# Attention of an encoder's first layer: items taken in pairs at set times instead of spread evenly

## The chip, the cores and the metric

The kernel runs on one core of a Trainium2 chip. The metric is the device time of one execution in microseconds (us), as the median of several runs. Engines are named as in the profile: PE (TensorE, matmuls and transposes; PEld is its weight load), DVE (VectorE), ACT (ScalarE), POOL (GpSimd), SP (SyncE, which issues the transfers).

## The reference

256 tokens of 1024 channels pass through two layers and a final norm; all is float32. The change is in the first ("even") layer, which runs two attentions side by side and projects both to the output:

```python
def even_mixer(xn, w_in, rpb, q_norm, w_uq, kv_norm, w_ukv, w_o, cos_r, sin_r):
    hcat = xn @ w_in
    a_qkv = hcat[..., :o0].reshape(b, s, 3, NA_HEADS, HEAD_DIM)
    out_a = neighbourhood_attention(a_qkv[:, :, 0], a_qkv[:, :, 1], a_qkv[:, :, 2], rpb)
    c_q = rms_norm(hcat[..., o0:o1], q_norm)
    c_kv = rms_norm(hcat[..., o1:o2], kv_norm)
    k_pe = apply_rope(hcat[..., o2:][:, :, None, :], cos_r, sin_r)
    q = (c_q @ w_uq).reshape(b, s, MLA_HEADS, MLA_NOPE + MLA_ROPE)
    q = jnp.concatenate([q[..., :MLA_NOPE], apply_rope(q[..., MLA_NOPE:], cos_r, sin_r)], axis=-1)
    kv = (c_kv @ w_ukv).reshape(b, s, MLA_HEADS, MLA_NOPE + MLA_V)
    ...
    out_b = dense_attention(q, k, v, (MLA_NOPE + MLA_ROPE) ** -0.5)
    return jnp.concatenate([out_a, out_b], axis=-1) @ w_o
```

Both attentions have 8 heads. The kernel computes the neighbourhood attention densely, with a bias table that carries the window; the other one ("MLA") has 96 channels per head for queries and keys and 64 for values. The second ("odd") layer and the two MLP blocks are as before in both kernels and come after the stretch that is changed.

## The kernel before

**Products.** A float32 operand is cut into a high half and the rest: `split` writes the high half on ACT (a CAST, L181) and the rest on DVE (a subtraction, L182). One product is then three matmuls (`mm3`, L185 to L187). `two_heads` (L194) does the same for two heads of 64 channels at once: they stand in two halves of PE's rows, which the trace shows as a 64*128 tile. The mix (L757) writes two heads into two halves of PE's columns, a 128*64 tile. All other matmuls and the transposes use the full array (128*128, or 96*128).

**Items.** The 16 items of the attention are 2 kinds x 4 pairs of heads x 2 tiles of 128 tokens. One item is: scores on PE; sn (a scaled copy and its row minimum) on DVE, L728 or L731; Exp on ACT, L733, one for each head; the reciprocal rz on DVE, L734; the scaling on ACT, L736, one for each head; four transposes on PE (`turn_probs`, L743); a copy of them to `pts` on ACT or DVE (L745), whichever the scheduler picks; the mix on PE (L757); and the split of the mix into oah/oal (first kind) or obh/obl (second kind), the operands of the output projection.

**Around them.** `main` lists the GEMM steps of the stretch with a cost in us each: the query and key projections of head pairs 1 to 3 (`qk_steps`), the MLA's up-projections (`kg`, `ug`: GEMM, copies to ktok and qtok, rotary embedding on DVE, L517 to L521) and their transposes (`kt`, `ut`, L649, split into kh/kl and qh/ql), and the first part of the output projection (`out_steps`). Its sum of costs serves as a clock: after each step the loop issues as many entries of `side`, the list of scores, turns and mixes, as keeps both lists in step. In `side` the scores of item n stand before the turn of item n-1 and the mix of item n-2. A scheduler then puts the instructions of each engine in a fixed order; `tc.high_priority` moves those inside it ahead. The banks of PSUM come from two tags, "acc" and "w"; the weights are split on ACT and DVE some steps ahead (whi, wlo).

Of the kernel before, what the change touches and what calls it, by code (L numbers as in the profile page):

```python
# [23 lines left out]
P = 128  # L24
D = 1024
KT = D // P
T = 256
NT = T // P
# [10 lines left out]
SPLIT_AHEAD = 2  # L39
WPARTS = 4  # L40
NORM_PRIO = 300

QK_ORDER = (0, 2, 1)

# [2 lines left out]
def trunk(ctx, tc, a, out):  # L47
    nc = tc.nc
# [8 lines left out]
    def scratch(shape, name):  # L57

        n = int(np.prod(shape))
        v = work.tile([P, 512], F32, tag="scratch", name=name, bufs=12)[:, :n]  # L60
        if len(shape) == 2:
            v = v.rearrange("p (a b) -> p a b", b=shape[1])
        return v
# [10 lines left out]
    def quarter_pair(name):  # L74
        return [act.tile([P, KT // 2, T], F32R, tag="quarter", name=name + v, bufs=4) for v in "hl"]

    def bank(tag):
        return ps.tile([P, 512], F32, tag=tag, name=tag)
# [101 lines left out]
    def split(hi, lo, src, eng=None):  # L180
        a = nc.scalar.copy(hi, src).ins  # L181
        return a, (eng or nc.vector).tensor_tensor(lo, src, hi.bitcast(F32), op=ALU.subtract).ins  # L182

    def mm3(o, sh, sl, mh, ml, first, last):
        nc.tensor.matmul(o, sh, mh, start=first, stop=False)  # L185
        nc.tensor.matmul(o, sh, ml, start=False, stop=False)  # L186
        nc.tensor.matmul(o, sl, mh, start=False, stop=last)  # L187

    def two_heads(o, hi, lo, ts):

        for n, (y, z) in enumerate(((hi, hi), (hi, lo), (lo, hi))):
            for j in range(2):
                pb = slice(64 * j, 64 * j + 64)
                nc.tensor.matmul(o[j], y[pb, 0, ts], z[pb, 1, :], start=n == 0, stop=n == 2)  # L194
# [10 lines left out]
    def tok(t):  # L205
        return slice(t * P, (t + 1) * P)
# [61 lines left out]
    def column(r, t):  # L268
        return r[:, t:t + 1]
# [8 lines left out]
    def join(b, o, n, xT):  # L278

        v = x[:, 2 * b:2 * b + 2, :]  # L280
        nc.vector.tensor_tensor(v, two(o), v, op=ALU.add)
        for f in zip(*(prepare(k, n, xT) for k in (2 * b, 2 * b + 1))):
            run_all(f)

    def hand_over(accs, last, n):

        xT, s = pair_tile(), sum_tile()
        for b in range(4):
            last[b]()
            with tc.high_priority(NORM_PRIO):  # L290
                join(b, accs[b], n, xT)
        return xT, s

    def hand_over_tokens(accs, last, n, scale):
# [4 lines left out]
        def leave(h, t):  # L299
            last(h, t)  # L300
            acc, sc = accs[2 * t + h], column(scale, t)
            with tc.high_priority(NORM_PRIO):
                y = ys[h, t] = scratch([512], "y")
# [3 lines left out]
        def turn(h):  # L307
            with tc.high_priority(NORM_PRIO):
                for b in range(2):
                    pt = bank("w")  # L310
                    for k in range(2):
                        for t in range(NT):
                            c = (2 * b + k) * P
                            nc.tensor.transpose(pt[:, k * T + t * P:k * T + (t + 1) * P], ys[h, t][:, c:c + P], ident)
                    join(2 * h + b, pt, n, xT)
# [21 lines left out]
    def out_steps(accs, mixed, wo, k):  # L337

        def step(fbs):
            if k // 2 not in wo:  # L340
                wo[k // 2] = weight()
            onto(accs, wo[k // 2], (k % 2) * D, (ALL, k % 4), mixed[k // 4], k == 0, k == KT - 1, fbs)
        return [lambda fbs=fbs: step(fbs) for fbs in (range(0, 4), range(4, 8))]
# [148 lines left out]
    def even(ep):  # L492
# [205 lines left out]


        mixed = [quarter_pair("oa"), None]  # L700
        items = [(0, t, hp) for hp in range(4) for t in range(NT)] + [(1, t, hp) for hp in range(4) for t in range(NT)]
        biases, probs, turned = {}, {}, {}

        def load_bias(n):
            if n < 8:
                _, t, hp = items[n]
                biases[n] = ep.tile([P, 2, T], F32, tag="bias", name="bias", bufs=2)
                nc.sync.dma_start(biases[n], a["rpb"][t, hp])

        def scores(n):  # L710
            kind, t, hp = items[n]
            load_bias(n + 2)

            sb = [bank("w")[:, 0:T] for _ in range(2)] if kind == 0 else bank("w").rearrange("p (j n) -> p j n", j=2)
            s_of = lambda j: sb[j] if kind == 0 else sb[:, j]
            if kind == 0:
                two_heads(sb, *qk[hp], tok(t))
            else:
                for j in range(2):
                    h = 2 * hp + j  # L720
                    (qh, ql), (kh, kl) = mT["q"], mT["k"]
                    mm3(sb[:, j], qh[0:96, h, tok(t)], ql[0:96, h, tok(t)], kh[0:96, h, :], kl[0:96, h, :], True, True)
            pp, sn = scratch([2, T], "pp"), scratch([2, T], "sn")
            mn, z, rz = (work.tile([P, 2], F32, tag=v, name=v, bufs=3) for v in ("mn", "z", "rz"))
            for j in range(2):
                o = s_of(j)
                if kind == 0:
                    nc.vector.tensor_tensor_reduce(out=sn[:, j], in0=o, in1=biases[n][:, j, :], op0=ALU.add, op1=ALU.min,  # L728
                                                   scale=-1.0, scalar=3e38, accum_out=mn[:, j:j + 1])
                else:  # L730
                    nc.vector.tensor_scalar(sn[:, j], o, -MLA_SCALE, None, ALU.mult, ALU.min, accum_out=mn[:, j:j + 1])  # L731
            for j in range(2):
                nc.scalar.activation(pp[:, j], sn[:, j], AF.Exp, bias=mn[:, j:j + 1], scale=-1.0, accum_out=z[:, j:j + 1])  # L733
            nc.vector.reciprocal(rz, z)  # L734
            for j in range(2):
                nc.scalar.activation(pp[:, j], pp[:, j], AF.Copy, scale=rz[:, j:j + 1])  # L736
            probs[n] = pp

        def turn_probs(n):
            pp = probs.pop(n)  # L740
            pt = bank("w")
            for b in range(4):
                nc.tensor.transpose(pt[:, b * P:(b + 1) * P], pp[:, b // 2, (b % 2) * P:(b % 2 + 1) * P], ident)  # L743
            turned[n] = scratch([4, P], "pts")
            nc.any.tensor_copy(out=turned[n], in_=pt.rearrange("p (b n) -> p b n", b=4))  # L745

        def mix(n):
            kind, t, hp = items[n]
            pts = turned.pop(n)
            if mixed[kind] is None:  # L750
                mixed[kind] = quarter_pair("ob")
            v = (vna, vml)[kind]
            pvo = bank("acc" if n < 6 else "w")
            for kk in range(NT):
                for j in range(2):
                    h = 2 * hp + j
                    nc.tensor.matmul(pvo[64 * j:64 * j + 64, 0:P], v[:, kk, h * 64:(h + 1) * 64], pts[:, 2 * j + kk, :],  # L757
                                     start=kk == 0, stop=kk == NT - 1)
            split(*(z[:, hp, tok(t)] for z in mixed[kind]), pvo[:, 0:P])

        def attention():

            out = []
            for n in range(len(items) + 2):
                for fn, m in ((scores, n), (turn_probs, n - 1), (mix, n - 2)):
                    if 0 <= m < len(items):
                        out.append(lambda fn=fn, m=m: fn(m))
                if n == 0:
                    out += [lambda: None] * 2
            return out  # L770

        (ug, ut), (kg, kt) = uq_steps(), ukv_steps()
        first = qk_steps(0)
# [12 lines left out]
        main = [(1.31, f) for c in range(1, 4) for f in qk_steps(c)]  # L786
# [4 lines left out]
                     (.98, ug[i(1, h)]), (.43, kt[i(1, h)]), (.43, ut[i(1, h)])]  # L791
        main += [(0, lambda: accs.extend(open_accs()))]
        main += [(1.3, f) for k in range(6) for f in out_steps(accs, mixed, wo, k)]
        side = attention()
        at = -5
        total = sum(c for c, _ in main) + at
        done = 0
        for c, f in main:
            f()
            at += c  # L800
            while done < len(side) and done * total < at * len(side):
                side[done]()
                done += 1
        return accs, out_last(accs, mixed, wo)


    def odd(op, xT, s):
# [46 lines left out]
        def qk_steps(d):  # L854
# [4 lines left out]
            def gemm(b, f, half):  # L859
# [9 lines left out]
                if half == 1:  # L869
                    with tc.high_priority(NORM_PRIO):  # L870
                        if f == 0:
# [40 lines left out]
        def attention(u, d):  # L912
# [36 lines left out]
            def mix(out_tag):  # L949
                pvo = [bank(out_tag) for _ in range(NT)]  # L950
                for i in range(NT):
# [4 lines left out]
                    for c in range(2):  # L956
                        qs = slice(64 * c, 64 * c + 64)
                        for j in range(2):
                            cs = slice(64 * j, 64 * j + 64)
                            nc.tensor.matmul(pvo[i][cs, qs], d["v12"][:, 2 * i + c, cs], turned[i, j][:, 2, qs], start=False, stop=c == 1)  # L960
                with tc.high_priority(NORM_PRIO):
                    for i in range(NT):
# [37 lines left out]
        mix = done.pop()  # L1000
        weave(qk_steps(nd) + all_values(nd, NORM_PRIO), steps + [nothing, lambda: mix("w")])
        steps = attend(7, nd)
# [111 lines left out]
```

## Time and profile before

| | before |
|---|---|
| median of 3 runs | 747.87 us (747.73 to 748.14) |
| profiled execution | 748.65 us |
| its span | 746.9 us |
| PE busy in the span | 739.0 us |
| DVE busy, ACT busy | 544.2 us, 484.8 us |
| the attention stretch | 39.3 to 108.6 us of the span |

The span is the time from the first to the last recorded instruction of the profiled execution; 1.75 us lie around it. The attention stretch runs from the first scores to the last mix. A start is counted from the beginning of the span. In a timeline the time from one instruction's start to the next one's (its pitch) tells more than the duration, since neighbours overlap.

### The profile page before, as it was taken

Reading aid. Unit: us, or ns where it says so; the run is one execution under the profiler, and the core shown is the slowest. Engines: PE = TensorE matmul, PEld = TensorE weight load, DVE = VectorE, ACT = ScalarE, POOL = GpSimd, SP = SyncE. Lnnn points to the kernel's source line nnn. Section 1 sums busy time; section 2 is a strip of 40 time slices with the busy share of each in tenths; the row PEclk is TensorE's granted clock in tenths of the full one; section 3 lists DMA queues with packets and bytes.
Section 4 is the critical chain, followed back from the end, with each engine's and each line's share of the span. In section 5 each row is a group of like instructions: output and inputs, shape, how many; then the busy total and the mean of one; then the engine's idle time right before and its main releaser. Section 6 shows DMA issues by size and latency. Waiting matters only on the chain.

```text
span 746.9 us, 12279 instructions
## 1 busy us (share of the span) xinstructions
PE 739.0 (99%) x4635; PEld 646.4 (87%) x4635; DVE 544.2 (73%) x1137; ACT 484.8 (65%) x1075; POOL 8.7 (1%) x20
## 2 busy tenths in 40 slices
PE   9999999999999999999999999999999999999996
PEld 6998998888888888889899899998998888888885
DVE  6778858766566666997888788888858765665664
ACT  6788967554554555677786877867856554554551
POOL 0100000000000001000000000000000000000000
PEclk9999999999999999999999999999999999999998
DMA  8763334464555545554645636445545555545501
GB/s 282 317 255 114 114 113 170 171 225 173 179 211 177 186 172 165 200 183 165 208 141 178 223 122 215 165 162 198 203 165 176 190 198 197 186 183 187 193 15 56
DMA packets 25163, 133.19 MB, mean 178 GB/s; under 512 B 3728, under 2 KB 4752, under 8 KB 12304
## 3 DMA queue, kind: packets, MB, share of 16 engines
q1 hardware_dynamic: 24960, 132.15, 50.1%
q8 instruction: 36, 0.59, 0.3%
q10 hardware_dynamic: 144, 0.26, 0.1%
q14 instruction: 23, 0.19, 0.1%
HBM read 127.16 MB, written 1.05 MB: 172 GB/s over the span
## 4 chain that ended last, share of the span: by engine, by line
PE 93%; DMA 3%; DVE 1%; issue 1%; SPq 1%; ACT 1%; POOL 0%; POOLq 0%; ACTq 0%
PE w L370 16%; PE acc L185 14%; PE acc L187 13%; PE acc L186 13%; PE acc L867 12%; PE w L371 8%; PE acc L868 6%; PE w L194 1%; PE w L945 1%; PE w L925 1%; PE w L743 1%; DMA gx<-in_gx 1%; DMA bias<-in_rpb 1%; DMA raw<-in_w_v 1%; PE w L757 1%
## 5 line engine op out<-in xcount | busy, mean ns | idle before, releaser
L182 DVE TENSOR_TENSOR wlo<-raw,whi 128x512 fp32r<-128x512 f32 (+3 forms) x487 | 306.6, 664 | 135.1 <-ACT whi L181 134.4
L181 ACT CAST whi<-raw 128x512 fp32r<-128x512 f32 (+3 forms) x487 | 264.3, 601 | 171.3 <-PE w L370 62.3
L370 PE MATMUL w<-pair,whi 128*128 128x512 f32 x512 | 182.2, 397 | 0.0
L371 PE MATMUL w<-pair,wlo 128*128 128x256 f32 x512 | 143.9, 281 | 0.0
L867 PE MATMUL acc<-pair,whi 128*128 128x512 f32 x384 | 139.4, 403 | 0.0
L370 PEld LDWEIGHTS w<-pair,whi 128*128 128x128 f32 x512 | 96.2, 188 | 23.2
L868 PE MATMUL acc<-pair,wlo 128*128 128x256 f32 x384 | 108.1, 282 | 0.0
L185 PE MATMUL acc<-whi,hh 128*128 128x512 f32 x250 | 98.1, 392 | 0.0
L187 PE MATMUL acc<-whi,hl 128*128 128x512 f32 x250 | 97.7, 391 | 0.0
L186 PE MATMUL acc<-wlo,hh 128*128 128x512 f32 x250 | 97.7, 391 | 0.0
L371 PEld LDWEIGHTS w<-pair,wlo 128*128 128x128 f32 x512 | 96.1, 188 | 0.9
L867 PEld LDWEIGHTS acc<-pair,whi 128*128 128x128 f32 x384 | 72.2, 188 | 16.2
L868 PEld LDWEIGHTS acc<-pair,wlo 128*128 128x128 f32 x384 | 72.2, 188 | 0.2 <-issue 0.2
L187 PEld LDWEIGHTS acc<-whi,hl 128*128 128x128 f32 x250 | 47.0, 188 | 9.9
L185 PEld LDWEIGHTS acc<-whi,hh 128*128 128x128 f32 x250 | 47.0, 188 | 9.8
L186 PEld LDWEIGHTS acc<-wlo,hh 128*128 128x128 f32 x250 | 47.0, 188 | 8.9
L185 PE MATMUL acc<-whi,pair 128*128 128x384 f32 x128 | 43.8, 342 | 0.0
L187 PE MATMUL acc<-whi,pair 128*128 128x384 f32 x128 | 43.1, 337 | 0.0
L186 PE MATMUL acc<-wlo,pair 128*128 128x384 f32 x128 | 43.1, 337 | 0.0
L374 ACT COPY side<-w 128x256 f32<-128x256 f32 x64 | 23.7, 370 | 22.1 <-PE w L371 22.1
L375 DVE TENSOR_TENSOR u<-w,side 128x256 f32<-128x256 f32 x64 | 27.0, 421 | 3.8 <-ACT side L374 3.0
L181 ACT CAST hh<-hsq 128x512 fp32r<-128x512 f32 x32 | 19.9, 621 | 10.2 <-DVE hsq L377 10.2
(215 smaller groups left out, 1112.3 us busy)
## 6 DMA issues: line engine op xcount, KB each, us to landing
raw<-in_w SPq DMA_DIRECT2D x64, 1024.0 KB, 4.8
raw<-in_w_oqk SPq DMA_DIRECT2D x24, 1024.0 KB, 5.0
raw<-in_w_ov SPq DMA_DIRECT2D x16, 768.0 KB, 4.4
raw<-in_w_qk SPq DMA_DIRECT2D x4, 1024.0 KB, 8.9
raw<-in_w_oe SPq DMA_DIRECT2D x4, 1024.0 KB, 5.2
sw<-qk SPq DMA_DIRECT2D x64, 64.0 KB, 2.4
raw<-in_w_oo SPq DMA_DIRECT2D x4, 1024.0 KB, 5.1
bias<-in_rpb SPq DMA_DIRECT2D x8, 256.0 KB, 4.2
```

Source lines behind the costliest of these rows:

```text
L181: a = nc.scalar.copy(hi, src).ins
L182: return a, (eng or nc.vector).tensor_tensor(lo, src, hi.bitcast(F32), op=ALU.subtract).ins
L185: nc.tensor.matmul(o, sh, mh, start=first, stop=False)
L186: nc.tensor.matmul(o, sh, ml, start=False, stop=False)
L187: nc.tensor.matmul(o, sl, mh, start=False, stop=last)
L194: nc.tensor.matmul(o[j], y[pb, 0, ts], z[pb, 1, :], start=n == 0, stop=n == 2)
L370: nc.tensor.matmul(two(pu[f]), w[0][:, c], xT[2][:, k], start=k == 0, stop=False)
L371: nc.tensor.matmul(pu[f][:, 0:T], w[1][:, c], xT[0][:, k, :], start=False, stop=k == KT - 1)
L374: nc.scalar.copy(side[:, f], pu[f][:, T:2 * T])
L375: nc.vector.tensor_tensor(u[:, f], pu[f][:, 0:T], side[:, f], op=ALU.add)
L867: nc.tensor.matmul(two(pq), wh[:, ws], xp[:, k], start=k == 0, stop=False)
L868: nc.tensor.matmul(pq[:, 0:T], wl[:, ws], xh[:, k, :], start=False, stop=k == KT - 1)
```

## The change

The items are ordered so that the two tiles of one pair of heads follow each other, as before, but eight times are written out by hand. At the time `PAIRS_AT[p]` of the clock of `main` the scores of both tiles of pair p are issued, then the mix of both tiles of pair p-1 into one bank of 256 columns, and one split of 128x256 in place of two of 128x128; that split is issued with high priority. The turns of the two tiles follow 2.0 and 3.2 us of the clock later.

```diff
+PAIRS_AT = (5.0, 9.2, 13.6, 18.0, 22.6, 26.9, 31.1, 35.2)
+PAIRS_END = 39.6
...
-        def mix(n):
-            kind, t, hp = items[n]
-            pts = turned.pop(n)
+        def mix(p, tag):
+
+            kind, _, hp = items[2 * p]
...
-            pvo = bank("acc" if n < 6 else "w")
-            for kk in range(NT):
-                for j in range(2):
-                    h = 2 * hp + j
-                    nc.tensor.matmul(pvo[64 * j:64 * j + 64, 0:P], v[:, kk, h * 64:(h + 1) * 64], pts[:, 2 * j + kk, :],
-                                     start=kk == 0, stop=kk == NT - 1)
-            split(*(z[:, hp, tok(t)] for z in mixed[kind]), pvo[:, 0:P])
+            pvo = bank(tag)
+            for n in (2 * p, 2 * p + 1):
+                pts, tk = turned.pop(n), tok(items[n][1])
+                for kk in range(NT):
+                    for j in range(2):
+                        h = 2 * hp + j
+                        nc.tensor.matmul(pvo[64 * j:64 * j + 64, tk], v[:, kk, h * 64:(h + 1) * 64], pts[:, 2 * j + kk, :],
+                                         start=kk == 0, stop=kk == NT - 1)
+            with tc.high_priority(NORM_PRIO):
+                split(*(z[:, hp, :] for z in mixed[kind]), pvo[:, 0:T])
...
-            for n in range(len(items) + 2):
-                for fn, m in ((scores, n), (turn_probs, n - 1), (mix, n - 2)):
-                    if 0 <= m < len(items):
-                        out.append(lambda fn=fn, m=m: fn(m))
-                if n == 0:
-                    out += [lambda: None] * 2
-            return out
+            for p, at in enumerate(PAIRS_AT):
+                tag = "acc" if p < 5 else "w"
+
+                def start(p=p, tag=tag):
+                    for n in (2 * p, 2 * p + 1):
+                        scores(n)
+                    if p:
+                        mix(p - 1, tag)
+                out.append((at, start))
+                out += [(at + d, lambda n=2 * p + k: turn_probs(n)) for k, d in enumerate((2.0, 3.2))]
+            return out + [(PAIRS_END, lambda: mix(len(PAIRS_AT) - 1, "w"))]
...
-        side = attention()
-        at = -5
-        total = sum(c for c, _ in main) + at
-        done = 0
+        side, at = attention(), 0
         for c, f in main:
             f()
             at += c
-            while done < len(side) and done * total < at * len(side):
-                side[done]()
-                done += 1
+            while side and side[0][0] <= at:
+                side.pop(0)[1]()
```

The lines behind the new constants stand 3 lower than before (L194 becomes L197, L743 becomes L746, L733 and L736 become L736 and L739), and the mix is L762 instead of L757. The number of PE's instructions is the same; ACT has 6 fewer and DVE 10 fewer. Behind the attention every engine's order is the same.

On PE, an item of the first pairs stood alone before. These rows of the kernel before are the mix of item 1 and the scores of item 4, with the projection's matmuls around them.

```order
L185 MATMUL acc<-pair,whi 128x256
L186 MATMUL acc<-pair,whi 128x256
L187 MATMUL acc<-pair,wlo 128x256
L757 MATMUL acc<-pts,vna 64x128 x4
L194 MATMUL w<-qk_h 128x256 x2
L194 MATMUL w<-qk_l,qk_h 128x256 x2
L194 MATMUL w<-qk_h,qk_l 128x256 x2
L185 MATMUL acc<-pair,whi 128x256
```

In the changed kernel the scores of pair 2 (items 4 and 5) and the mix of pair 1 make one block on PE:

```order
L197 MATMUL w<-qk_h 128x256 x2
L197 MATMUL w<-qk_l,qk_h 128x256 x2
L197 MATMUL w<-qk_h,qk_l 128x256 x2
L197 MATMUL w<-qk_h 128x256 x2
L197 MATMUL w<-qk_l,qk_h 128x256 x2
L197 MATMUL w<-qk_h,qk_l 128x256 x2
L762 MATMUL acc<-pts,vna 64x128 x8
L188 MATMUL acc<-pair,whi 128x256
```

So twelve score matmuls and eight of the mix now stand together, where each item's six and four stood apart.

One pair later, on PE, the block of pair 3 (the scores of items 6 and 7, and the mix of pair 2) does not stay together in the changed kernel. The MLA's up-projections (384 columns) and single matmuls of scores and mix alternate:

```order
L197 MATMUL w<-qk_h,qk_l 128x256 x2
L762 MATMUL acc<-pts,vna 64x128 x4
L188 MATMUL acc<-whi,ch 128x384
...
L197 MATMUL w<-qk_h 128x256
L197 MATMUL w<-qk_l,qk_h 128x256
L197 MATMUL w<-qk_h,qk_l 128x256
L762 MATMUL acc<-pts,vna 64x128
L197 MATMUL w<-qk_h 128x256
L197 MATMUL w<-qk_l,qk_h 128x256
L197 MATMUL w<-qk_h,qk_l 128x256
L762 MATMUL acc<-pts,vna 64x128 x3
```

The second item's scores are issued one head at a time there, and the mix in pieces of 4, 1 and 3 matmuls. Then come the rest of the up-projections with eight transposes (L652), and the turns of items 6 and 7:

```order
L190 MATMUL acc<-whi,cl 128x384
L746 MATMUL w<-ident,pp 128x128 x4
L652 MATMUL w<-ident,qtok 96x128 x4
L746 MATMUL w<-ident,pp 128x128 x4
L652 MATMUL w<-ident,ktok 96x128 x4
L188 MATMUL w<-kh,qh 128x256
```

Between the two turns stands the transpose of qtok (L652), which was not next to them before; no main matmul is left between them and the first MLA scores (L188, kh and qh).

On ACT, at the same place in the kernel before (numbers behind a name tell buffers apart), the split's cast of one item and then the Exp of the next item:

```order
L181 CAST kh_858<-w_931 96x4x128 [waits PE_49]
L181 CAST oah_370<-acc_960 128x128 [waits PE_49]
L733 ACTIVATE pp_919,z_922<-sn_920,mn_921 128x256 [waits DVE_49] x2
L689 COPY ktok_942<-acc_938 128x4x64
L181 CAST qh_887<-w_953 96x4x128 [waits PE_49]
L667 COPY qtok_974<-acc_967 128x4x64 [waits PE_49]
L736 ACTIVATE pp_919<-pp_919,rz_923 128x256 [waits DVE_49]
```

And in the changed kernel, from the last rows before the cast of pair 2's mix to the scaling of item 7 (935 is item 6, 955 is item 7):

```order
L692 COPY ktok_923<-acc_919 128x4x64 [waits PE_49]
L184 CAST oah_370<-acc_967 128x256 [waits PE_49]
L736 ACTIVATE pp_935,z_938<-sn_936,mn_937 128x256 [waits DVE_49] x2
L184 CAST qh_888<-w_978 96x4x128 [waits PE_49]
L736 ACTIVATE pp_955,z_958<-sn_956,mn_957 128x256 [waits DVE_49,Activation_49]
L739 ACTIVATE pp_935<-pp_935,rz_939 128x256 [waits DVE_49]
L739 ACTIVATE pp_935<-pp_935,rz_939 128x256 [waits Activation_49]
L736 ACTIVATE pp_955,z_958<-sn_956,mn_957 128x256
L670 COPY qtok_992<-acc_985 128x4x64
L184 CAST kh_866<-w_1000 96x4x128 [waits PE_49]
L739 ACTIVATE pp_955<-pp_955,rz_959 128x256 [waits DVE_49]
```

The cast waits for the whole mix of pair 2 and stands ahead of all four Exps of pair 3; the copy qtok_992, which the transpose between the two turns needs, stands behind them.

## Rows read from the trace of the kernel before

**Rows 1.** The page: busy time of the engines, and the chain that ended last.

```profile
PE 739.0 (99%) x4635; PEld 646.4 (87%) x4635; DVE 544.2 (73%) x1137; ACT 484.8 (65%) x1075; POOL 8.7 (1%) x20
...
PE 93%; DMA 3%; DVE 1%; issue 1%; SPq 1%; ACT 1%; POOL 0%; POOLq 0%; ACTq 0%
```

**Rows 2.** Windows: stretch, its length, busy us, granted clock, DMA share, GB/s.

```profile
39.30:108.60 69.30, 69.30 (x597) 60.87 (x596) 53.18 (x170) 58.79 (x168) 1.17 (x4) 1.00 0.44 160
730.00:747.00 17.00, 10.88 (x65) 9.54 (x64) 7.43 (x15) 3.36 (x9) 1.22 (x2) 0.88 0.16 62
```

**Rows 3.** Timeline of PE (start, duration): scores between full-array matmuls.

```profile
39.00 0.28 PE L186 MATMUL acc<-pair,whi 128*128 128x256 f32 x1
39.11 0.28 PE L187 MATMUL acc<-pair,wlo 128*128 128x256 f32 x1
39.31 0.38 PE L194 MATMUL w<-qk_h 64*128 64x256 f32 x2
...
39.86 0.38 PE L185 MATMUL acc<-pair,whi 128*128 128x256 f32 x1
40.09 0.28 PE L186 MATMUL acc<-pair,whi 128*128 128x256 f32 x1
```

**Rows 4.** Timeline of PE: a mix and scores behind it, without a break.

```profile
52.48 0.28 PE L187 MATMUL acc<-pair,wlo 128*128 128x256 f32 x1
52.69 0.66 PE L757 MATMUL acc<-pts,vna 128*64 128x128 f32 x8
53.28 0.38 PE L194 MATMUL w<-qk_h 64*128 64x256 f32 x2
...
53.82 0.38 PE L185 MATMUL acc<-pair,whi 128*128 128x256 f32 x1
```

**Rows 5.** Timeline of PE: a mix in two pieces, then one in a piece.

```profile
82.84 0.43 PE L757 MATMUL w<-pts,vml 128*64 128x128 f32 x2
83.20 0.44 PE L743 MATMUL w<-ident,pp 128*128 128x128 f32 x2
83.57 0.65 PE L757 MATMUL w<-pts,vml 128*64 128x128 f32 x6
84.15 0.39 PE L185 MATMUL w<-kh,qh 96*128 96x256 f32 x1
...
87.13 0.66 PE L757 MATMUL w<-pts,vml 128*64 128x128 f32 x8
87.71 0.39 PE L185 MATMUL w<-kh,qh 96*128 96x256 f32 x1
```

**Rows 6.** Timelines, one item: its scores on PE, its first sn on DVE.

```profile
45.37 0.39 PE L194 MATMUL w<-qk_h 64*128 64x256 f32 x2
...
46.10 0.42 DVE L728 CUSTOM_DVE_ANT_0 sn<-w,bias 128x256 f32<-128x256 f32 x1
```

**Rows 7.** Timeline of ACT; the bracket is the idle time before, and what ended it.

```profile
39.35 1.02 ACT L181 CAST whi<-raw 128x256 fp32r<-128x256 f32 x3 [0.23 <-ACT whi L181]
...
64.41 0.27 ACT L181 CAST oah<-acc 128x128 fp32r<-128x128 f32 x1 [0.66 <-PE acc L757]
64.57 0.51 ACT L733 ACTIVATE pp<-sn,mn 128x256 f32<-128x256 f32 x1
...
65.07 0.50 ACT L733 ACTIVATE pp<-sn,mn 128x256 f32<-128x256 f32 x1
...
65.82 0.59 ACT L181 CAST qh<-w 96x512 fp32r<-96x512 f32 x1
66.29 0.38 ACT L667 COPY qtok<-acc 128x256 f32<-128x256 f32 x1
66.56 0.92 ACT L736 ACTIVATE pp<-pp,rz 128x256 f32<-128x256 f32 x2
```

**Rows 8.** Timeline of DVE: rest of kh, then a rotary embedding up to the next sn.

```profile
64.06 0.68 DVE L182 TENSOR_TENSOR kl<-w,kh 96x512 fp32r<-96x512 f32 x1
...
67.04 0.28 DVE L517 TENSOR_TENSOR r<-acc,cosr 128x128 f32<-128x128 f32 x1
...
67.50 0.41 DVE L728 CUSTOM_DVE_ANT_0 sn<-w,bias 128x256 f32<-128x256 f32 x1
```

More of the change, by code (lines that the diff above doesn't have):

```diff
@@ L700, in even @@
         mixed = [quarter_pair("oa"), None]
-        items = [(0, t, hp) for hp in range(4) for t in range(NT)] + [(1, t, hp) for hp in range(4) for t in range(NT)]
+        items = [(kind, t, hp) for kind in range(2) for hp in range(4) for t in range(NT)]
         biases, probs, turned = {}, {}, {}
@@ L800, in even @@
             at += c
-            while done < len(side) and done * total < at * len(side):
-                side[done]()
-                done += 1
+            while side and side[0][0] <= at:
+                side.pop(0)[1]()
+        assert not side
         return accs, out_last(accs, mixed, wo)
```

## The prediction

> **What bounds the kernel now.** I read the page first. PE is busy 739.0 of 746.9 us, and 93% of the chain that ended last is PE's [rows 1]. Then the windows: in the stretch of the attention, 39.3 to 108.6 us, PE is busy all 69.30 us at a granted clock of 1.00, while ACT has 58.79 and DVE 53.18 us of work [rows 2]. So PE sets the time of this stretch, and ACT and DVE matter only where they let PE wait, which they don't do now. Behind the stretch PE's order is unchanged and it has nothing to make up for a delay, so that I let what PE gains or loses here shift the end one for one. The change must pay in PE's own time, and may cost in waits that don't exist yet.
>
> PE's matmuls are the same before and after. What differs is how often it changes the shape of its tiles, so I read PE's timeline next, from start to start.
>
> **What it removes: changes of tile shape.** A full-array matmul of 256 columns takes .11 us (39.00 to 39.11). Before scores it takes .20 (39.11 to 39.31), the six of them take .55 (39.31 to 39.86) where three pairs, two heads in parallel, would be .34 at .11, and the first full one behind them takes .23 (39.86 to 40.09) [rows 3]. So an excursion to the scores' shape costs .09 + .21 + .12 = **.42 us** more than its work. For the mix: .21 before it (52.48 to 52.69), .59 for it (52.69 to 53.28) [rows 4] or .58 (87.13 to 87.71) [rows 5] where four pairs at .11 would be .44; with .11 behind it, as behind the scores, it makes .10 + .15 + .11 = **.36 us**. Mix and scores in a row share one exit: .10 from the full shape, .15 in the mix, then .54 instead of .34 for the scores (53.28 to 53.82) [rows 4] and .12 behind them, in all **.57 us**. A mix that is cut in two leaves a matmul without its partner: .36 (82.84 to 83.20) and .58 (83.57 to 84.15) [rows 5], .94 instead of .58; beside the second entry and exit that is .21 to .22 of lost parallel work.
>
> Before, 5 scores stand alone, 3 stand behind a mix, and 12 mixes stand alone, with one more in two pieces: 5 x .42 + 3 x .57 + 14 x .36 is 8.85 us, near the 9.0 that I get with the changes inside one block counted one by one. After, pair 0 is one excursion (.42), pairs 1 and 2 are scores with a mix behind them (.57 each), pair 3 and its mix make six alternations (scores with mix .57, then scores, mix, scores and mix of .3 to .4 each), and pair 4 cuts its mix in two, pair 5 too, and pairs 6 to 8 have one mix each. I count 30 changes against 47, 6.3 us with .8 of work that loses its partner. **The removal is worth 9.0 - 6.3 = 2.7 us.** A sum of what each block of the stretch takes above its nominal pitches gives 10.6 us, of which 1.6 belongs to other things; I take 2.7 and no more.
>
> The splits: 16 of 128x128 become 8 of 128x256. On ACT that is .16 each (64.41 to 64.57) against .31 (three in .93 and one overlap, 1.02) [rows 7], so nothing to be gained; on DVE a little. ACT and DVE are off the path, so this counts as nothing, hidden by PE's 69.3 us against their 58.8 and 53.2 [rows 2]. If that cover were gone it would still be worth under 1 us in all.
>
> **What it adds: the softmax of two items at once.** In pairs 0 to 2 both items' scores end within 1.1 us, and four Exps at .50 (64.57 to 65.07) and four scalings at .41 (two in .92) [rows 7] follow, with the cast of the mix, .31, ahead of them. The first sn starts .73 behind the scores' start (45.37 to 46.10) and takes .42 [rows 6]. That makes the first transposes possible about .73 + .42 + two or three Exps + .31 + other casts, 3.6 to 3.7 us behind the pair's first score, with the second half .41 later; PE, with the matmuls that stand between at .11 each, comes there after 3.5 to 3.8. That is too close to tell. The bounds for each of the six turns are 0 (the scaling is ready) and .5 (PE comes as the first scaling starts, and waits for a whole one); I take the middle, .25, for **1.5 us**.
>
> **Pair 3** is where I find a real wait. ACT's row there has the cast of pair 2's mix ahead of all Exps of pair 3. PE reaches the end of that mix late, because the order puts up-projections between its pieces: from the turn of item 5 to the mix's end I add four transposes at .11, three matmuls of 512 columns at .23 and five of 384 at .17 (by columns, from .11 for 256), three blocks of scores at .55 [rows 3] and the mix's pieces at .36, .36 and .58 [rows 5], with two entries from the full shape at .20: 5.1 by these, and 5.5 with the exits, which I take. ACT's work from there is kh (.47, 65.82 to 66.29), pts about the same, qtok .27 (66.29 to 66.56) and two ktok near it [rows 7], and three casts of weights near .52, in all 3.3 us. So ACT stands about 2 us at the cast, with Exps behind it whose sn is there. The row of before shows the same wait in small: the cast of 64.41 was preceded by .66 us of idle time, ended by PE's mix, and the Exp started right behind it, at 64.57 [rows 7].
>
> From the start of that cast on, ACT runs cast .31, two Exps (1.3), qh .47 (1.8), the third Exp (2.3), two scalings (3.1), the fourth Exp (3.6), qtok (3.9), kh (4.4). DVE then has the reciprocal of item 7, r1 and r2 (.46, 67.04 to 67.50), the rest of kh (.68) [rows 8] and only then the sum that finishes qtok, so this is there at 5.3. PE meanwhile has 2.9 us of other work (seven matmuls of 384 columns, three of 512, eight transposes, one exit), turns item 6 at 2.8 to 3.5 with a wait of .25, and then wants the transposes of qtok: **PE waits about 1.85 us** there, with nothing else in its row. What is queued behind it: the turn of item 7 and the transposes of ktok, then the MLA's scores, so everything shifts. Bounds: nothing, if ACT is itself so late that it comes to the cast with the mix; 2.5, if kl takes DVE first and the cast starts with the mix's end.
>
> The Trainium skill, in Perfetto Trace Analysis, section Tensor Engine Instruction, says that PE may pull weight loads ahead but that ACT and DVE run strictly in order. By that rule the Exps stay behind the cast and the sum holds; were they able to pass it, the 1.85 would fall away and the sum would be near -1.2. The idle time of 64.41 agrees with the rule [rows 7], and the sum goes by that row.
>
> In the second half, pairs 4 to 8, I find .3 us: the turn of item 8 is ready 3.06 after the mix of pair 3, and PE comes after 3.15.
>
> **The sum** on the profiled execution's own 748.65 us (its span of 746.9 and 1.75 around): -2.7 + 1.5 + .25 + 1.85 + .3 = +1.2. Since PE's blocks ran 1.6 us longer than the pitches that I added, ACT gets that time too; I give back .5 of it: **+0.7 us**, 749.35. The median of the runs shown is 747.87, .78 below that execution, so **748.6 us**.
>
> **Rivals.** (A) The forecast, about no change. Its own range: 746.5 (no waits in pairs 0 to 2, pair 3 near 1) to 749.3 (all of them as taken, nothing given back, and a little more). .42.
>
> (B) The softmax keeps pace: ACT comes late to the cast of pair 2, so that it doesn't stand there, and the turns find their scalings ready. For it: ACT has only 58.8 us of work in 69.3 [rows 2]. Against it: the idle .66 in before, at the same place [rows 7]. Waits of .7 in all, -2.7 + .7 = -2.0: 745.9; with none 745.2. .30.
>
> (C) Slower: the cast that stands ahead of Exps does so in pair 4 as well. The margin there is 3.15 - 3.06 = .09; with one cast of qh or kh (.47) ahead of the Exps it becomes a wait of .4 to .8 at the turns of items 8 and 9 each, and then the turns of pairs 0 to 2 would hardly be at .25 but near .5. That is +.7 + 2 x .4 to .8 + up to 1.5, of which I take half the last two: +2.5, 750.4, at most 750.8. It decides from the point where the turn of item 8 is ready later than 3.15 behind the mix. .24.
>
> (D) The clock falls. The granted clock is 1.00 in the stretch, and .88 in the last 17 us, where PE was busy only 10.88 [rows 2]: .12 x 17 is 2.0 us of full speed lost, so about 4 us at the lower level of 1.2 GHz. If the 2 us wait of pair 3 let it fall for as long, with PE busy behind it, that would be +2.0 on top of A: 750.6. .04. The Trainium skill, in TensorE: Matmul & The Clock Gate, section HAM oscillation, warns of waits that let the clock fall to its lower level and have to be paid again; by it D would be the outcome wherever the wait is long enough, and of the waits here only pair 3's could be.
>
> **How the numbers follow.** About .2% (1.5 us) tells from no change: 746.4 to 749.4. B is faster, .30. A is the same, .42. C and D are slower, .28. For 8 in 10 the range must reach into B and C: from 745.3, where B has almost no waits, to 750.8, the bound of C. That leaves out about a tenth at each end, and the unknown costs (0 to .5 at six turns, 0 to 2.5 in pair 3) lie inside.
>
> **What would show it.** In the changed kernel's trace PE should have its first idle time of this stretch. Right: at the transposes of qtok between the turns of items 6 and 7 one gap of 1 to 2.5 us, its releaser DVE's qtok; ACT idle about 2 us at the cast of 128x256 in front of it; the blocks of pairs 1 and 2 (scores, scores, mix) without full-array matmuls inside; PE's stretch from the first scores to the last mix 69 to 71 us. Wrong: no gap at that place, or ACT's cast without idle time (then B); gaps of over .4 us at the turns of items 0 to 5, 8 and 9 (then C); a clock below 1.00 in a window of 39 to 109 us (then D). If the changes of shape cost as much per block after as before, in rows like those of [rows 3 to 5], then the 2.7 is wrong and the kernel slower than A by as much. If the end does not shift with the stretch, the way in which I let PE's time count is wrong.

## The result

The changed kernel took 750.35 us in the median of 6 runs (749.7 to 751.42), the one before 747.9 (747.73 to 748.14). The ratio is 1.0034, with a 95% interval of 1.0023 to 1.0045: slower, by more than the .2% that tells from no change.

The six times are two groups: 749.7, 749.73 and 749.83, and 750.86, 751.21 and 751.42. The profiled execution, 749.7, is of the lower one. Its page, with engines and chain as in [rows 1]:

```profile
PE 737.5 (99%) x4635; PEld 647.5 (87%) x4635; DVE 542.1 (72%) x1127; ACT 484.6 (65%) x1069; POOL 8.7 (1%) x20
...
PE 91%; DMA 3%; ACT 2%; DVE 1%; issue 1%; SPq 1%; POOL 0%; POOLq 0%; ACTq 0%; DVEq 0%
```

ACT is now in the chain with 2%, where it had 1%, and PE's part has fallen by 2. The window of the attention stretch, which answers to [rows 2], says the same: PE no longer fills it, and the granted clock is 1.00.

```profile
39.30:110.00 70.70, 68.56 (x597) 61.44 (x596) 50.83 (x160) 58.00 (x162) 1.17 (x4) 1.00 0.45 157
```

To compare two executions I take the time between two instructions of PE on either side of the stretch that stand in both programs: the transposes of cn, ahead of it, and the first matmul of the MLP behind it. Timeline of the kernel before, these two:

```profile
34.77 0.52 PE L556 MATMUL w<-ident,cn 128*128 128x128 f32 x3 [0.18 <-DVE cn L548]
...
114.39 0.40 PE L370 MATMUL w<-pair,whi 128*128 128x512 f32 x1
```

And of the changed kernel:

```profile
34.36 0.52 PE L559 MATMUL w<-ident,cn 128*128 128x128 f32 x3 [0.62 <-DVE cn L551]
...
115.32 0.39 PE L373 MATMUL w<-pair,whi 128*128 128x512 f32 x1
```

The stretch took 79.62 us (114.39 - 34.77) and now takes 80.96 (115.32 - 34.36), 1.34 more. The profiled execution of before came .41 late into it (34.77 against 34.36), so that 1.34 - .41 = .93 of the 1.05 between the two profiled times (749.7 and 748.65) comes from here: the end shifts with the stretch, as the forecast assumed.

**Where PE waits now.** The waits of PE in 36 to 120 us (before, the same view had no row):

```profile
PE w L652 <- DVE qtok L524: 1.9, 1, 1.9
PE w L746 <- ACT pp L739: 0.3, 1, 0.3
```

The timeline of PE shows the place, and the blocks that answer to [rows 3 to 5]: the turns of pairs 0 to 2, the block of pair 1's scores with the mix of pair 0, then pair 3.

```profile
42.74 0.84 PE L746 MATMUL w<-ident,pp 128*128 128x128 f32 x4
44.79 0.71 PE L746 MATMUL w<-ident,pp 128*128 128x128 f32 x4
46.81 0.39 PE L197 MATMUL w<-qk_h 64*128 64x256 f32 x2
...
47.72 1.09 PE L762 MATMUL acc<-pts,vna 128*64 128x128 f32 x16
48.74 0.38 PE L188 MATMUL acc<-pair,whi 128*128 128x256 f32 x1
...
50.79 0.44 PE L746 MATMUL w<-ident,pp 128*128 128x128 f32 x2 [0.29 <-ACT pp L739]
...
58.06 0.84 PE L746 MATMUL w<-ident,pp 128*128 128x128 f32 x4
60.48 0.75 PE L746 MATMUL w<-ident,pp 128*128 128x128 f32 x4
```

Four transposes that wait for nothing take .60 (L652 at 73.07 in the next view). Turns of .84, .71, .84 and .75 are turns that stood still between their instructions, though only one gap, .29, is printed as idle: at the first, ACT's two scalings take 42.19 to 43.08, and the second of them ends .34 after PE's first transpose started. The block of pair 1 runs from 46.81 to 48.74 without a full-array matmul inside, as the order says. Pair 3, on PE:

```profile
62.90 0.66 PE L762 MATMUL acc<-pts,vna 128*64 128x128 f32 x8
...
64.57 0.38 PE L197 MATMUL w<-qk_h 64*128 64x256 f32 x1
...
65.11 0.43 PE L762 MATMUL acc<-pts,vna 128*64 128x128 f32 x2
65.48 0.38 PE L197 MATMUL w<-qk_h 64*128 64x256 f32 x1
...
66.02 0.65 PE L762 MATMUL acc<-pts,vna 128*64 128x128 f32 x6
...
69.50 0.83 PE L746 MATMUL w<-ident,pp 128*128 128x128 f32 x4
72.18 0.61 PE L652 MATMUL w<-ident,qtok 128*96 128x128 f32 x4 [1.85 <-DVE qtok L524]
...
73.07 0.60 PE L652 MATMUL w<-ident,ktok 128*96 128x128 f32 x4
```

ACT at the same place, to be read beside [rows 7]: the cast of the mix was preceded by 2.66 us of idle time that the mix ended, and all Exps of pair 3 stand behind it; qtok's copy comes 3.5 us after the cast.

```profile
63.67 0.38 ACT L692 COPY ktok<-acc 128x256 f32<-128x256 f32 x1
66.71 0.37 ACT L184 CAST oah<-acc 128x256 fp32r<-128x256 f32 x1 [2.66 <-PE acc L762]
66.98 0.51 ACT L736 ACTIVATE pp<-sn,mn 128x256 f32<-128x256 f32 x1
...
69.74 0.50 ACT L736 ACTIVATE pp<-sn,mn 128x256 f32<-128x256 f32 x1
...
70.23 0.35 ACT L670 COPY qtok<-acc 128x256 f32<-128x256 f32 x1
70.49 0.58 ACT L184 CAST kh<-w 96x512 fp32r<-96x512 f32 x1
```

And DVE, beside [rows 8]: the reciprocal, the rotary embedding, the rest of kh, and only then the sum that PE wants.

```profile
70.36 0.17 DVE L737 RECIPROCAL rz<-z 128x2 f32<-128x2 f32 x1 [1.11 <-ACT pp L736]
70.69 0.29 DVE L520 TENSOR_TENSOR r<-acc,cosr 128x128 f32<-128x128 f32 x1 [0.16 <-ACT qtok L670]
70.90 0.35 DVE L522 TENSOR_TENSOR r<-acc,sinr 128x64 f32<-128x64 f32 x2
71.16 0.68 DVE L185 TENSOR_TENSOR kl<-w,kh 96x512 fp32r<-96x512 f32 x1
71.76 0.28 DVE L524 TENSOR_TENSOR qtok<-r,r 128x128 f32<-128x128 f32 x1
```

The sum ends at 72.04, 5.33 after the cast's start. The wait is the one that was forecast, in place, releaser and length. What it does not explain is the upper group of times.

### The profile page after: what moved, and what is told of

Its sections match the earlier page's. It is cut to its first block, busy times and chain, and to the rows that moved or that the text cites. A ratio compares the mean times of both kernels' runs of the same rounds, so it can differ in the third digit from the quotient of the medians.

```text
span 747.9 us, 12265 instructions
## 1 busy us (share of the span) xinstructions
PE 737.5 (99%) x4635; PEld 647.5 (87%) x4635; DVE 542.1 (72%) x1127; ACT 484.6 (65%) x1069; POOL 8.7 (1%) x20
## 3 DMA queue, kind: packets, MB, share of 16 engines
HBM read 127.16 MB, written 1.05 MB: 171 GB/s over the span
## 4 chain that ended last, share of the span: by engine, by line
PE 91%; DMA 3%; ACT 2%; DVE 1%; issue 1%; SPq 1%; POOL 0%; POOLq 0%; ACTq 0%; DVEq 0%
PE w L373 16%; PE acc L188 13%; PE acc L190 13%; PE acc L189 13%; PE acc L875 12%; PE w L374 8%; PE acc L876 6%; PE w L953 1%; PE w L197 1%; PE w L933 1%; PE w L746 1%; DMA bias<-in_rpb 1%; DMA gx<-in_gx 1%; DMA raw<-in_w_v 1%; PE acc L963 1%
## 5 line engine op out<-in xcount | busy, mean ns | idle before, releaser
L188 PE MATMUL acc<-whi,hh 128*128 128x512 f32 x250 | 98.1, 393 | 0.0
L188 PEld LDWEIGHTS acc<-whi,hh 128*128 128x128 f32 x250 | 47.0, 188 | 9.9
L188 PE MATMUL acc<-whi,pair 128*128 128x384 f32 x128 | 43.8, 342 | 0.0
```

## The experiments

Each time is a median, with the kernel before run beside it on the same chip (medians of 748.1, 748.04 and 748.13). "The stretch" is the interval above: 79.62 before, 80.96 in the changed kernel's profile.

### The changed kernel again

No edit.

> The changed kernel itself once more, to see whether its runs again fall into two groups (749.7 to 749.8 and 750.9 to 751.4 before) and what a second profile shows of the difference. If the 1.4 us between the groups come from the start of the program (the first weights landing .85 us later, as in the profiled execution of the kernel before), the kernels that share this call should show the same two groups, 1 us or more apart. If they come from the attention, the wait at the transposes of qtok should differ between the two profiles of this kernel. Median expected: 750.3.

Ten runs: 749.3 to 749.71 (six) and 750.52 to 751.46 (four), median 749.67, ratio 1.0028 (1.0019 to 1.0038), where 750.3 was expected: the median follows from how many runs fall into either group. Two kernels without a long wait of PE, run beside it, have no such gap: before (747.66 to 748.66) and the one with priority on qtok, below. The profile (749.47) was again of the lower group, with a stretch of 80.93 and a wait of 1.8 at qtok. Its first projection ran .6 later than in the first profile (at 22 us), and at the transposes of cn it was .2 ahead: what the start loses, the wait for cn takes up. So the start of the program makes neither group.

Two more profiled executions, one run each:

> The changed kernel again, one profiled execution, to catch one of the upper group (about 751) in a profile; two such looks were at 749.7 and 749.5 with a granted clock of 1.00 from 70 to 80 us. Clock theory: an execution near 751 shows a granted clock of .80 to .90 in 70 to 80 us, right behind the wait at the transposes of qtok, and PE's matmuls at twice their pitch there; an execution near 749.6 shows 1.00. Rival (the group comes from elsewhere): an execution near 751 shows 1.00 in that stretch, and loses its time at another place.

> As the look before, the same kernel and the same two outcomes: near 751 with a granted clock of .80 to .90 in 70 to 80 us, or near 749.6 with 1.00 (clock theory); near 751 with 1.00 (rival).

Both were of the upper group, 750.74 and 751.4, with stretches of 82.53 and 82.57. Windows of the second (stretch, length, busy us of PE, PEld, DVE, ACT and POOL, granted clock, DMA share, GB/s):

```profile
72.00:74.00 2.00, 1.74 (x9) 1.73 (x10) 0.54 (x2) 1.34 (x4) 0.29 (x1) 0.56 0.00 0
74.00:76.00 2.00, 2.00 (x12) 1.97 (x11) 1.79 (x6) 0.80 (x2) 0.00 (x0) 0.59 0.05 12
76.00:78.00 2.00, 2.00 (x22) 1.56 (x21) 1.44 (x6) 0.00 (x0) 0.00 (x0) 1.00 0.00 0
```

And its timeline of PE from the wait on:

```profile
72.26 1.06 PE L652 MATMUL w<-ident,qtok 128*96 128x128 f32 x4 [1.85 <-DVE qtok L524]
73.11 1.06 PE L746 MATMUL w<-ident,pp 128*128 128x128 f32 x4
73.97 1.06 PE L652 MATMUL w<-ident,ktok 128*96 128x128 f32 x4
...
75.25 0.41 PE L190 MATMUL w<-kh,ql 96*128 96x256 f32 x1
75.47 0.37 PE L188 MATMUL w<-kh,qh 96*128 96x256 f32 x1
75.67 0.28 PE L189 MATMUL w<-kl,qh 96*128 96x256 f32 x1
```

The wait is the same 1.85. Behind it the four transposes take 1.06 instead of .60 and a matmul of 256 columns .41 instead of .28, until about 75.5, where the clock is back. In 72 to 76 the granted clock was .56 and .59, that is 1.2 GHz for most of it. Both stretches are 1.6 longer than those of the lower group (80.96 and 80.93), all of it in this place. The clock theory holds for these two executions. By their time, 9 of the 18 runs of this kernel were of the upper group; that the clock fell in the other seven too is inferred from their time. The mean granted clock of a whole execution can't settle it, as it lies at .995 to .999 in the upper group and at .997 to .999 in the lower one.

### The wait filled with work

```diff
             pt = bank("w")
+            if (n, t, h) == ("q", 1, 0):
+                for _ in range(7):
+                    nc.tensor.matmul(pt, warm[:, 0:P], warm, start=True, stop=True)
             for i in range(4):
                 nc.tensor.transpose(pt[0:96, i * P:(i + 1) * P], src[:, i, :], ident)
```

> The changed kernel with seven extra matmuls (bfloat16, 512 columns, of a zero tile; they write into the bank of qtok's transposes, which overwrite it, and are not part of the computation) ahead of the transposes at which PE waited 1.85 us. So PE works where it stood still; the scheduler puts the turn of item 7 ahead of them as well. Clock theory (the upper group of the changed kernel's runs, about 1.3 us above the lower, is TensorE's clock falling to 1.2 GHz after that wait in some executions, as in the profile without the priority, where the granted clock was .50 in 74 to 76 us): the upper group disappears, all runs within 1 us, median 749.4 to 750. Rival (the groups come from transfers or from the start of the program): the groups stay, with runs at 750.5 to 751.5.

749.46, all eleven runs between 748.85 and 749.67, ratio 1.0018 (1.0009 to 1.0026). No upper group any more, and the level is that of the lower one: the stretch is 80.75 at a granted clock of 1.00, though PE does seven matmuls more, and PE's only printed wait is the .29 of pair 1. The time at qtok is lost as before; what the filling takes away is the second price.

### Without the priority of the mix's split

```diff
-            with tc.high_priority(NORM_PRIO):
-                split(*(z[:, hp, :] for z in mixed[kind]), pvo[:, 0:T])
+            split(*(z[:, hp, :] for z in mixed[kind]), pvo[:, 0:T])
```

> The changed kernel without the high priority of the mix's split, all else as it is. In ACT's row the cast of pair 2's mix still stands ahead of the four Exps of pair 3, and the copy of qtok stands behind even more of them. Theory (the wait of 1.85 us comes from four Exps and the scalings of two items ahead of qtok, and from the late mix): the wait at the transposes of qtok stays at 1.5 to 2.5 us, time 750 to 751. Rival (the priority makes the wait, by pulling the cast ahead of ready work): the wait falls under .5 and the time to 748.5.

752.37 (750.42 to 753.96), ratio 1.0059 (1.0045 to 1.0072), stretch 83.62. So a wait of this size needs no priority, and the rival falls. The time was above what I expected, and the wait stood elsewhere than I had said: PE's row now has the mix of item 6 between the two turns, and ACT copies its pts only behind the scalings, qtok and kh.

```profile
69.49 0.77 PE L746 MATMUL w<-ident,pp 128*128 128x128 f32 x4
72.80 1.03 PE L762 MATMUL acc<-pts,vna 128*64 128x128 f32 x8 [2.55 <-ACT pts L748]
```

2.55 us of waiting; and the clock fell in this profile too. The window behind it:

```profile
74.00:76.00 2.00, 2.00 (x9) 1.77 (x10) 0.00 (x0) 0.55 (x2) 0.00 (x0) 0.50 0.00 0
```

### The priority alone, in the kernel before

```diff
-            split(*(z[:, hp, tok(t)] for z in mixed[kind]), pvo[:, 0:P])
+            with tc.high_priority(NORM_PRIO):
+                split(*(z[:, hp, tok(t)] for z in mixed[kind]), pvo[:, 0:P])
```

> The kernel before with the high priority on each item's own split, and nothing of the pairs. One part of the change alone. Theory (the priority by itself neither costs nor gains, since PE doesn't wait in the kernel before): 747.7 to 748.4. Rival (a cast that stands ahead of Exps makes PE wait): 748.8 or more, with a wait at a turn.

748.14, ratio .9998 (.9989 to 1.0007), stretch 79.59, no wait of PE. In the order of before, this part of the change is worth nothing by itself.

### Priority on qtok

```diff
-                nc.scalar.copy(s[:, :, 0:64], pq4[:, :, 0:64])
-                rope(s[:, :, 64:96], pq4[:, :, 64:96], 4, cosr[:, t, :], sinr[:, t, :], 16)
+                with tc.high_priority(NORM_PRIO):
+                    nc.scalar.copy(s[:, :, 0:64], pq4[:, :, 0:64])
+                    rope(s[:, :, 64:96], pq4[:, :, 64:96], 4, cosr[:, t, :], sinr[:, t, :], 16)
```

> The changed kernel with the copy of qtok and its rotary embedding issued with the same priority as the mix's split. The row of ACT then has qtok's copy behind the third Exp of pair 3 instead of behind the fourth and the scalings of item 6, and DVE's sum stands ahead of the reciprocal of item 7 and of kl. Theory A (PE waits only because qtok's sum stands behind kl and a reciprocal): the wait of 1.85 falls to under .3 and comes back nowhere: 748.5. Theory B (ACT is behind by its idle time at the cast, whatever stands last): qtok's wait goes, and .8 to 1.5 us of it come back at the turn of item 7: 749.4 to 750.

747.82 (747.38 to 748.35), ratio .9997 (.9988 to 1.0006), with no upper group; stretch 79.25, 1.71 under the changed kernel's. That is .7 under the time of theory A and 1.6 under that of B. PE's waits in 36 to 120 us are

```profile
PE w L747 <- ACT pp L740: 0.4, 2, 0.3
PE acc L763 <- DVE pts L749: 0.3, 1, 0.3
```

and nothing near 1.85 came back at the turn of item 7; the scheduler moved that turn behind other work. It moved more than that: the mix of pair 2 ends earlier on PE, as its last eight matmuls now stand in one piece ahead of the last scores. PE, ACT twice and DVE:

```profile
64.72 0.66 PE L763 MATMUL acc<-pts,vna 128*64 128x128 f32 x8
...
65.42 0.37 ACT L184 CAST oah<-acc 128x256 fp32r<-128x256 f32 x1 [1.39 <-PE acc L763]
...
68.81 0.35 ACT L671 COPY qtok<-acc 128x256 f32<-128x256 f32 x1
...
69.85 0.29 DVE L524 TENSOR_TENSOR qtok<-r,r 128x128 f32<-128x128 f32 x1
```

qtok's sum ends at 70.14 instead of 72.04, 1.90 earlier (the stretches of both begin within .02 us of each other). Of that, 1.29 is the cast, which starts at 65.42 instead of 66.71; the copy is only .13 nearer to the cast (3.39 behind it instead of 3.52), and the sum .48 nearer to the copy, with kl no longer ahead of it. So the edit removes the wait, but it doesn't separate theory A from a mix that ends earlier. The same edit in the kernel before:

> The kernel before with the priority on the copy of qtok and its rotary embedding, the edit that took 1.9 us off the changed kernel. Theory (the edit only removes the wait that the pairs made): no wait is there to remove, time as before, 747.8 to 748.4. Rival (the edit helps by itself, whatever the items' order): 746.5 to 747.4, and then the pairs alone cost as much as ever.

747.86, ratio .9996 (.9988 to 1.0005), stretch 79.53. The edit is worth something only where the pairs had made a wait.

### Pair 3 earlier

```diff
-PAIRS_AT = (5.0, 9.2, 13.6, 18.0, 22.6, 26.9, 31.1, 35.2)
+PAIRS_AT = (5.0, 9.2, 13.6, 17.3, 22.6, 26.9, 31.1, 35.2)
```

> The changed kernel with pair 3 issued at 17.3 instead of 18.0 of the clock of main. PE's row then has the scores of both items and the mix in three blocks (9 scores and 4 of the mix, 3 scores and 4 of the mix) instead of six, and the up-projections' matmuls stand between the turn of item 6 and the transposes of qtok. Theory (most of the loss is the wait in pair 3, since nothing else is left in PE's row there): waits of pair 3 fall from 2.2 to under .7, two changes of shape fewer (.3): 748.3 to 748.9. Rival (the loss is spread over the turns of all pairs, or lies in what the pairs do to ACT): 749.8 to 750.5.

749.15 (748.3 to 750.3), ratio 1.0014 (1.0005 to 1.0023), stretch 80.38. Neither expectation: the wait at qtok is gone, but 1.16 us stand at a mix that waits for the copy of its turn on ACT, .5 at transposes of ktok and .3 at later ones. Two of its eleven runs lie apart, at 750.23 and 750.3, with the lowest mean granted clock (.995; the others .997 to .999); the profile, 749.15, is not one of them. With both edits, qtok's priority and pair 3 at 16.7:

> The changed kernel with the priority on qtok and with pair 3 issued at 16.7 instead of 18.0: its block is 9 scores and 4 of the mix, then 3 scores and 4 of the mix, and up-projections stand around the turn of item 6. Theory (the pairs save some 2 us of shape changes, and what is left of the waits in pair 3 is .5): 747.2 to 747.6, waits in pair 3 under .3. Rival (waits come back at another place of pair 3, as ACT has the same work there): 747.8 to 748.5.

746.71 (746.48 to 747.32), ratio .9982 (.9973 to .9991), stretch 78.29. That is under the range of the theory, and the only version here that beats both kernels. Its waits:

```profile
PE acc L763 <- DVE rz L738: 0.4, 1, 0.4
PE w L747 <- ACT pp L740: 0.3, 1, 0.3
```

### One item's softmax at a time

```diff
-                    for n in (2 * p, 2 * p + 1):
-                        scores(n)
+                    scores(2 * p)
...
+                out += [(at + 1.2, lambda p=p: scores(2 * p + 1))]
```

> The changed kernel with the scores of a pair's second item issued 1.2 of the clock behind those of the first, the mix and its one split still for the pair. The softmax then has one item at a time. More excursions for scores: pair 0 two instead of one, pair 3 two of six (none by single heads), pairs 1 and 2 keep theirs in one block or add one. Theory (the loss is the waits that two items at once bring, most of it at qtok): no wait over .5 in PE's row, time 747.6 to 748.3. Rival (the waits come from the mix's late block and its cast, which stays): a wait of 1 us or more near the turns of pair 3, time 749 to 750.

748.4 (747.98 to 749.14), ratio 1.0005 (.9996 to 1.0014), stretch 79.84. The long wait is gone; one of .63 at the turn of item 5 is there. Nearer to the theory than to the rival, but .1 above the range that I gave it. And the rival's condition did not stay: the cast of pair 2's mix starts at 65.67 instead of 66.71, with .49 of idle time ahead of it instead of 2.66. So this run doesn't separate the two either.

### Turns later

The version with both edits, with turns at 2.6 and 3.8:

```diff
-                out += [(at + d, lambda n=2 * p + k: turn_probs(n)) for k, d in enumerate((2.0, 3.2))]
+                out += [(at + d, lambda n=2 * p + k: turn_probs(n)) for k, d in enumerate((2.6, 3.8))]
```

> The pairs with the priority on qtok, pair 3 at 16.7, and the turns at 2.6 and 3.8 instead of 2.0 and 3.2 of the clock behind a pair's scores. In pairs 1 and 4 to 7 full-array matmuls then stand where PE met the transposes too early; for the mix the copies of the turns come .6 later. Theory (what is left of the waits are turns that come .1 to .5 before their scaling is ready, about 1 us in all): 746.0 to 746.6, below the 746.71 with turns at 2.0 and 3.2. Rival (a later turn makes the mix wait for its copy, and what one gains the other takes): 746.6 to 747.5.

751.02 (750.39 to 752.76), ratio 1.0045 (1.0032 to 1.0058): a miss of both. The profile is a run of 752.52, with a stretch of 84.06. The scheduler laid out pair 3 anew: PE waits .71 at transposes of ktok ahead of the pair, then .30 at a turn, .66 at transposes of ktok and .86 at the mix of item 6, which waits for its copy; behind that the clock falls. PE's timeline and a window behind it:

```profile
69.51 0.84 PE L747 MATMUL w<-ident,pp 128*128 128x128 f32 x4 [0.30 <-ACT pp L740]
...
71.00 0.61 PE L652 MATMUL w<-ident,ktok 128*96 128x128 f32 x4 [0.66 <-issue]
72.48 0.43 PE L763 MATMUL acc<-pts,vna 128*64 128x128 f32 x2 [0.86 <-DVE pts L749]
...
74.00:76.00 2.00, 2.00 (x10) 1.20 (x9) 1.47 (x5) 0.80 (x3) 0.06 (x1) 0.50 0.03 8
```

## Why the prediction was right and where it was not

**The range and the verdict.** 750.35 lies inside 745.3 to 750.8. The likeliest number, 748.6 with no change, was 1.8 too low, and the outcome (slower by .34%) had .28. That the range holds is in part luck: its upper end was drawn for case C, which did not happen, case A's own range ended at 749.3, below even the lower three of the six runs, and none of the six lies within .5 of 750.35, the middle of the gap between the groups.

**The wait in pair 3** was read from the order and priced from rows, and it came out: 1.85 us, released by qtok's sum on DVE, with ACT idle at the cast ahead of it. That idle time was 2.66 instead of about 2, which changes nothing, as the price counts from the cast's start (5.33 to the sum's end, where 5.3 was forecast). The chain is there link by link in the rows above: the mix that ends late, the cast that waits for it, four Exps and two scalings ahead of qtok's copy on ACT, kl ahead of the sum on DVE, and PE, which starts .14 after the sum's end. ACT and DVE kept to their order, as the sum assumed. How the 1.85 divides among the links is not shown. The edit on qtok takes 1.71 us off the stretch (and .09 in the kernel before), but it ended the mix 1.29 earlier as well. In the other runs without the long wait (pair 3 at 17.3 or 16.7, one item at a time) the cast comes .9 to 1.9 us earlier in the stretch too, and where it stays late (67.11, without the priority of the split) a long wait stays.

**The turns of pairs 0 to 2** were put at 1.5 us. By the lengths of the turns above against .60, with the .29 and what stands at 50.79 around it, I count about 1.4. The single turns run from .1 to more than .5, so the .25 taken for each is right in the sum and not turn by turn. The turn of item 6 took .23 more than an undisturbed one, for .25.

**The shape changes** were put at 2.7 us. Counted block by block in both timelines (from the full-array matmul ahead of a block to the one behind it, less the pitches of the work itself), the 47 changes of before cost 8.6 us and the 30 of the changed kernel 6.2, so 2.4 came back. The counts were right, and so was the 6.3 for after: the block of pair 1, from 46.81 to 48.74, costs .58 where .57 was forecast. What was too high is before, 9.0. With the waits that makes 1.85 + .23 + 1.4 - 2.4 = +1.1, and about .25 of the 1.34 that the stretch is longer has no row of its own.

**The terms that failed** in the lower group are small: the .3 for pairs 4 to 8 (no wait is printed there, and its two times, 3.06 and 3.15, stood without their rows) and the .5 that I gave back because PE's blocks run longer than their pitches. Without the second the sum would have been +1.2, beside 1.34 measured in the stretch.

**The case that was too cheap** is D, the clock, with .04. Its price, +2.0 on top of A, was near (1.6 measured in two executions), and so was its place, directly behind pair 3's wait. Its chance was wrong by far: half of the runs, 9 of 18, show it by their time, and both profiles from that half by their granted clock. With half the runs 1.6 higher, the median of the first six runs fell between the groups. The rule of the Trainium skill that the prediction named under D (TensorE: Matmul & The Clock Gate, section HAM oscillation) spoke against the change; the two executions with a fallen clock agree with it, the two at 1.00 behind the same wait do not. I had given it almost no chance, though the sum itself held the wait behind which it happens.

**Case C** did not happen: no wait at the turns of items 8 and 9. That the kernel is slower, as C had it, comes from A's waits and from D together: the lower group alone (median 749.55 against 748.1 in the ten runs) and the kernel with the wait filled (749.46 against 748.04) are .2% above before, at the edge of what counted as no change, and D takes the median past it. **Case B**, in which ACT doesn't stand idle at the cast, did not happen either, and its 745.9 was not reached even without the wait: 747.82 with qtok's priority, 746.71 with pair 3 at 16.7 as well.

## What to carry to other kernels

Where PE is never idle, putting work of one kind together saves changes of tile shape, some .4 us for each way there and back here, but it also puts the ACT and DVE work of two items into one queue, and a small copy that stands behind them (here qtok) becomes what PE waits for. Read the order of the other engines for what stands behind the bundle, and for the late result that the bundle itself waits for. Giving the copy that PE needs next priority was worth 1.7 us here, more than half of what the bundling saves; but the scheduler answered by ending the mix 1.3 us earlier too, so read the new order before crediting the edit. A wait of 2 us in a PE-bound stretch may be paid twice, since the clock can fall behind it, in some executions and not in others; two groups of times are the sign.

## What was not expected of the hardware

After one wait of 1.85 us on PE the granted clock fell to 1.2 GHz for about 3 us in two of four profiled executions of the same program (.56 and .59 in two windows of 2 us of one of them, against 1.00 in the other two), and the price was 1.6 us; by their times, half of 18 runs paid it. After a wait of 2.55 us it fell as well in the one profile. In the one profile of the version with later turns it fell where no single wait was longer than .86 (.30, .66 and .86 between 69.2 and 72.5 us; .50 in 74 to 76 us). Where seven matmuls on zeros stood in the wait, none of eleven runs lay in the upper group.
